# Neighbourhood attention with projections one step ahead instead of two, and rotated queries of the first layer written directly into their tile

## The chip, the core and the metric

One core of a Trainium2 chip runs the whole program. The metric is the device time of one execution in microseconds (us). Five engines work side by side, each with its own queue of instructions that it runs strictly in order: PE (TensorE, matrix products into PSUM), DVE (VectorE), ACT (ScalarE), POOL (GpSimd) and SP (SyncE, which here issues the DMAs). An instruction that waits on a semaphore holds back all that stands behind it on its engine.

## The reference, cut to what matters

Two layers of a backbone over 1024 latent tokens and 256 context tokens, width 1024, all in float32. The first layer runs differential attention (8 heads; each with two query/key halves of 64 columns, values of 128) beside a short convolution. The second runs two-dimensional neighbourhood attention beside a gated linear attention. What the change touches is this:

```python
q = apply_rope(aq.reshape(bsz, seq, *qk_shape), cos, sin)      # layer 0, latent tokens only
q = cp[2].reshape(bsz, clen, *qk_shape)                        # layer 0, context tokens: no rotation
...
s_loc = einsum(q_r, k_band) * scale + bias                     # layer 1: 8 rows x 16 columns around each query
s_ctx = einsum(q_r, kc) * scale                                # and all 256 context keys
p = softmax(concat([s_loc, s_ctx]))
out = p_loc @ v_band + p_ctx @ vc
```

In layer 1 the queries, keys and values are projections `h @ w_in` of the normed tokens, 16 heads of 64 columns.

## The kernel before, in words

**Matmul in pieces.** A float32 operand is split into a high part and a rest (`whi`/`wlo` for weights by `split_w`, L241 on ACT and L242 mostly on POOL; `hA`/`hB` for tokens), and a product is the sum of three products. A projection unit turns 128 columns of weights over all tokens; it has a step for each chunk of tokens (512, 512, 256). A step is `proj_chunk` (L438): 24 matmuls into one of two PSUM banks called `pj`, which the step's `use` function then empties.

**The stream.** `Stream` holds all projection units of the program in order. Attention code asks it for steps between its own pieces: `ws.run(n)` issues n steps, `ws.until(name)` all up to a named one, `ws.open(gate)` needs all before a gate to be done. So attention (many short, dependent pieces on four engines) and projections (long, independent PE work) are interleaved. The Tile scheduler then orders the instructions of each engine by priority and readiness, so a piece may move some way from where the code put it.

**Layer 0, the rotation.** At the start of a head `diff_head` calls `ws.until("v..")`, which runs the projections of keys, queries and values one after the other. For keys and queries `rope` (L514) copies the PSUM bank into a scratch tile `ropex` (L519, ACT), swaps lanes (L521, DVE), multiplies by cosine (L522, DVE) and sine (L523, POOL) and adds (L524, DVE, into the scratch tile). `use_q` (L538) then copies the scratch to the query tile `qf` (L543, POOL), for all three chunks; the context chunk is only scaled, not rotated. The first scores of the head need `qd`, the split queries (L581 on ACT, L582 and L583 on DVE), which read `qf`.

**Layer 1, neighbourhood attention.** `na` walks over 64 units: 8 pairs of heads i, 2 heads m in each, 4 blocks bp of 256 queries. For a unit, `scores` builds the split queries `nqd` (L1459 on ACT, L1461 and L1462 on DVE) from the projected queries `nq` (L1393), multiplies with the keys into PSUM (`NS`, L1473 and L1474, twice, once for each 128 queries), adds the bias and takes the maximum (`np`, L1477 on DVE), exponentiates (L1479, ACT), takes the reciprocal (L1480, DVE) and scales (L1481, POOL). `values` transposes the weights (`ntr`, L1522, PE), splits them (`pth` L1531 on ACT, `ptl` L1532 on DVE) and multiplies with the values (`nav`, L1499); the last sum of a unit is `nu` (L1505, DVE). The order in the code is: scores of unit n+1, values of unit n, then one projection step for the pair i+1 (keys `ck` 3 steps, values `cv` 3, queries `cq` 2: 8 steps for 8 units). Ahead of the loop stands `ws.run(2)`. On POOL the same stretch has also the bias tiles `nB` (L1433), the copies of the keys `nk` (L1387), the gate product `nu` (L1546) after each pair and `wlo` (L242) once for each unit of weights. After unit 53 the projections have run out; the steps of the output projection (`ops`, L756) come with unit 59.

Of the kernel before, what the change touches and what calls it, by code (L numbers as in the profile page):

```python
# [10 lines left out]
F32 = mybir.dt.float32  # L11
F32R = mybir.dt.float32r
AF = mybir.ActivationFunctionType
ALU = mybir.AluOpType
# [4 lines left out]
P = 128  # L19
D = 1024  # L20
NK = D // P
SEQ = 1024
CTX = 256
TOK = SEQ + CTX
# [74 lines left out]
class Kernel:  # L99
# [411 lines left out]
        rope_es.close()  # L511
        return conv_es

    def rope(self, ps, t0, tn, scale):  # L514

        nc = self.nc
        big = self.ap.tile([P, 1280], F32, name="ropex", tag="p0", bufs=2)
        x, s = big[:, 0:tn], big[:, 640:640 + tn]
        nc.scalar.mul(out=x, in_=ps, mul=scale) if scale != 1.0 else nc.scalar.copy(out=x, in_=ps)  # L519
        if t0 < SEQ:  # L520
            nc.vector.stream_shuffle(s, x, [i ^ 16 for i in range(32)])  # L521
            nc.vector.tensor_tensor(out=x, in0=x, in1=self.cos[:, t0:t0 + tn], op=ALU.mult)  # L522
            nc.gpsimd.tensor_tensor(out=s, in0=s, in1=self.sin[:, t0:t0 + tn], op=ALU.mult)  # L523
            nc.vector.tensor_tensor(out=x, in0=x, in1=s, op=ALU.add)  # L524
        return x, s

    def use_k(self, h, ci, t0, tn, ps):
# [8 lines left out]
            nc.vector.tensor_tensor(out=self.kst[m][64:128, t0:t0 + tn], in0=x[half], in1=hi[half], op=ALU.subtract)  # L536

    def use_q(self, h, ci, t0, tn, ps):  # L538
        nc, ap = self.nc, self.ap
        if ci == 0:  # L540
            self.qf = ap.tile([P, TOK], F32, name="qf", tag="qf")
        x, _ = self.rope(ps, t0, tn, 0.125)
        nc.gpsimd.tensor_copy(self.qf[:, t0:t0 + tn], x)  # L543

    def use_v(self, h, ci, t0, tn, ps):
        nc, ap = self.nc, self.ap
# [892 lines left out]
    def na(self):  # L1439
        nc, ap, ws = self.nc, self.ap, self.ws  # L1440
# [108 lines left out]
        bias[0] = self.na_bias(0)  # L1549
        units = [(i, m, bp) for i in range(8) for m in range(2) for bp in range(4)]  # L1550
        nxt = scores(*units[0])
        ws.run(2)
        for n, (i, m, bp) in enumerate(units):
            ps_ = nxt
            if bp == 1 and 2 * i + m < 15:
# [93 lines left out]
```

## Time and profile before

| | |
|---|---|
| Median of 3 runs | 3112.27 us (3111.68 to 3113.80) |
| The profiled execution | 3112.84 us, its span 3111.1 us |
| Busy share of the span | PE 95%, DVE 61%, ACT 49%, POOL 31% |
| Mean granted TensorE clock | 0.985 |
| Layer 0's attention | about 140 to 1400 us |
| Neighbourhood attention | about 2300 to 2940 us |

PE is busy nearly throughout, so the end moves when PE's idle time does, when its instructions become fewer, or when its clock changes. The views below are read for PE's idle time: how much of it lies in the two stages that the change touches, and what ended each stretch of it.

### The profile page before, as it was taken

What the parts mean: (1) busy time and instruction counts of PE and PEld (TensorE: products, weight loads), DVE (VectorE), ACT (ScalarE), POOL (GpSimd) and SP (SyncE); (2) the same over time, 40 slices, a digit from 0 to 9 for tenths busy, and PEclk for the clock granted to TensorE, in tenths of its full rate; (3) what the DMA queues carried; (4) which work ended last, traced back from release to release, by engine and by line L of the source; (5) the groups of instructions that cost most, each with busy time, mean ns of one, the idle gap of its engine ahead of it and who ended that gap; (6) DMA issues with size and microseconds to landing.
All of it is one profiled execution on the core that took longest, in us unless ns stands there. A gap on an engine that the chain in (4) does not pass through costs nothing. (4 is left out here: it accounts for less than half of the span.)

```text
span 3111.1 us, 42394 instructions
## 1 busy us (share of the span) xinstructions
PE 2948.6 (95%) x16244; PEld 2463.5 (79%) x16244; DVE 1890.8 (61%) x3157; ACT 1523.8 (49%) x2821; POOL 972.7 (31%) x765
## 2 busy tenths in 40 slices
PE   6999999999999999999999999999999999998898
PEld 4888888888888887888787787878777777777786
DVE  5675757575665657564245757575847666667723
ACT  4553535353544454444345665555635554555621
POOL 3212131313121211215333232222336545555622
PEclk9999999999999999999999999999999999999999
DMA  6111110211110201125432112121121111112323
GB/s 226 34 45 48 48 51 29 64 35 58 35 58 28 72 28 56 36 63 192 136 124 73 51 44 66 58 62 55 55 71 38 44 37 38 43 43 98 102 90 122
DMA packets 236982, 206.53 MB, mean 66 GB/s; under 512 B 43591, under 2 KB 194538, under 8 KB 236778
## 3 DMA queue, kind: packets, MB, share of 16 engines
q1 hardware_dynamic: 236778, 203.81, 21.2%
q8 instruction: 128, 2.10, 0.3%
q14 instruction: 76, 0.62, 0.1%
HBM read 168.10 MB, written 35.67 MB: 65 GB/s over the span
## 5 line engine op out<-in xcount | busy, mean ns | idle before, releaser
L242 POOL TENSOR_TENSOR wlo<-wraw,whi 128x1024 fp32r<-128x1024 f32 x149 | 368.8, 2475 | 1164.1 <-ACT whi L241 1045.0
L438 PE MATMUL pj<-hBh,whi 128*128 128x512 f32 (+1 forms) x1712 | 386.2, 354 | 8.2 <-ACT hBh L353 4.8
L438 PE MATMUL pj<-hBl,whi 128*128 128x512 f32 (+1 forms) x1712 | 364.4, 348 | 0.9 <-DVE hBl L354 0.9
L438 PE MATMUL pj<-hBh,wlo 128*128 128x512 f32 (+1 forms) x1712 | 348.1, 344 | 0.0
L241 ACT CAST whi<-wraw 128x1024 fp32r<-128x1024 f32 x176 | 184.7, 1049 | 318.0 <-PE ops L756 188.6
L438 PEld LDWEIGHTS pj<-hBh,whi 128*128 128x128 f32 x1712 | 276.8, 192 | 42.4 <-ACT hBh L353 5.4
L438 PEld LDWEIGHTS pj<-hBl,whi 128*128 128x128 f32 x1712 | 279.4, 191 | 36.8 <-DVE hBl L354 1.1
L438 PEld LDWEIGHTS pj<-hBh,wlo 128*128 128x128 f32 x1712 | 277.2, 190 | 37.2
L438 PE MATMUL pj<-hAh,whi 128*128 128x512 f32 x968 | 283.1, 414 | 14.7 <-ACT ropex L519 13.0
L438 PE MATMUL pj<-hAl,whi 128*128 128x512 f32 x968 | 255.4, 396 | 0.0
L594 DVE TENSOR_REDUCE st<-S 128x1 f32<-128x1280 f32 (+1 forms) x160 | 203.9, 1274 | 79.0 <-PE S L592 79.0
L438 PE MATMUL pj<-hAh,wlo 128*128 128x512 f32 x968 | 250.4, 397 | 0.0
L596 ACT ACTIVATE p<-S,st 128x1280 f32<-128x1280 f32 (+1 forms) x160 | 186.0, 1163 | 81.9 <-DVE st L594 80.4
L1481 POOL TENSOR_TENSOR np<-np,nst 128x640 f32<-128x640 f32 x128 | 168.1, 1315 | 143.5 <-DVE nst L1480 79.9
L438 PEld LDWEIGHTS pj<-hAh,wlo 128*128 128x128 f32 x968 | 182.4, 190 | 37.5
L438 PEld LDWEIGHTS pj<-hAh,whi 128*128 128x128 f32 x968 | 173.4, 194 | 48.5 <-ACT ropex L519 14.4
L438 PEld LDWEIGHTS pj<-hAl,whi 128*128 128x128 f32 x968 | 180.5, 191 | 35.7 <-issue 0.4
L592 PE MATMUL S<-kst,qd 128*128 128x512 f32 (+1 forms) x832 | 192.2, 360 | 0.2 <-ACT p L596 0.2
L1477 DVE CUSTOM_DVE_ANT_0 np<-NS,nB 128x640 f32<-128x640 f32 x128 | 105.0, 820 | 115.0 <-PE NS L1474 96.3
L592 PEld LDWEIGHTS S<-kst,qd 128*128 128x128 f32 x832 | 137.0, 188 | 40.3 <-ACT p L596 21.5
L617 ACT CAST ath<-atr 128x512 fp32r<-128x512 f32 (+1 forms) x208 | 99.1, 505 | 113.4 <-PE atr L614 112.8
L1531 ACT CAST pth<-ntr 128x512 fp32r<-128x512 f32 (+2 forms) x224 | 101.2, 461 | 84.2 <-PE ntr L1522 46.4
(361 smaller groups left out, 6266.5 us busy)
## 6 DMA issues: line engine op xcount, KB each, us to landing
wraw<-in_ev_w_in_dram SPq DMA_DIRECT2D x64, 512.0 KB, 4.0
wraw<-in_od_w_in_dram SPq DMA_DIRECT2D x56, 512.0 KB, 3.8
wraw<-in_w_out_dram SPq DMA_DIRECT2D x55, 512.0 KB, 3.8
wraw<-in_w_mod_dram SPq DMA_DIRECT2D x48, 512.0 KB, 3.6
sgT<-gt SPq DMA_DIRECT2D x32, 256.0 KB, 2.3
uT<-sg SPq DMA_DIRECT2D x8, 640.0 KB, 3.5
nG<-in_rpbp_dram SPq DMA_DIRECT2D x128, 40.0 KB, 2.2
xt<-in_x_dram SPq DMA_DIRECT2D x8, 512.0 KB, 6.6
```

What stands on the lines that cost most here:

```text
L241: nc.scalar.copy(out=hi, in_=u.raw)
L242: (nc.vector if u.lo_eng == "v" else nc.gpsimd).tensor_tensor(out=lo, in0=u.raw, in1=hi.bitcast(F32), op=ALU.subtract)
L438: nc.tensor.matmul(ps[:, 0:tn], lhsT=a[:, k, :], rhs=self.h_at(k, t0, tn)[b], start=n == 0, stop=n == 23)
L592: nc.tensor.matmul(S[:, c0:c0 + tn], lhsT=qd[:, 2 * m + part, P * qt:P * qt + P], rhs=self.kst[m][:, t0:t0 + tn], start=part == 0, stop=pa ...
L594: nc.vector.tensor_reduce(out=st[:, m:m + 1], in_=S[:, 0:n], axis=AX.X, op=ALU.max, negate=True)
L596: nc.scalar.activation(out=p[m][:, 0:n], in_=S[:, 0:n], func=AF.Exp, bias=st[:, m:m + 1], accum_out=st[:, 2 + m:3 + m])
L617: nc.scalar.copy(out=dh, in_=tv)
L1477: nc.vector.tensor_tensor_reduce(out=p, in0=S[:, z0:z0 + 640], in1=bias[2 * i + m][:, c0:c0 + 640], scale=1.0, scalar=3e38, op0=ALU.add, o ...
L1481: nc.gpsimd.tensor_tensor(out=p, in0=p, in1=st[:, 2:3].broadcast_to([P, 640]), op=ALU.mult)
L1531: nc.scalar.copy(out=hv[:, s:e], in_=tr[:, s:e])
```

## The change

In layer 0, `rope` takes an optional output. For rotated chunks the last addition on DVE writes its result straight to `qf`; the context chunk is scaled by ACT from PSUM straight into `qf`, with no scratch tile. The 24 POOL copies (three chunks, eight heads) are gone. In layer 1, `ws.run(2)` ahead of the loop becomes `ws.run(1)`, so each of the 56 projection steps is issued one unit later.

```diff
-    def rope(self, ps, t0, tn, scale):
+    def rope(self, ps, t0, tn, scale, out=None):
         nc = self.nc
+        if out is not None and t0 >= SEQ:
+            nc.scalar.mul(out=out, in_=ps, mul=scale)
+            return
...
-            nc.vector.tensor_tensor(out=x, in0=x, in1=s, op=ALU.add)
+            nc.vector.tensor_tensor(out=x if out is None else out, in0=x, in1=s, op=ALU.add)
         return x, s
...
     def use_q(self, h, ci, t0, tn, ps):
-        nc, ap = self.nc, self.ap
         if ci == 0:
-            self.qf = ap.tile([P, TOK], F32, name="qf", tag="qf")
-        x, _ = self.rope(ps, t0, tn, 0.125)
-        nc.gpsimd.tensor_copy(self.qf[:, t0:t0 + tn], x)
+            self.qf = self.ap.tile([P, TOK], F32, name="qf", tag="qf")
+        self.rope(ps, t0, tn, 0.125, self.qf[:, t0:t0 + tn])
...
         nxt = scores(*units[0])
-        ws.run(2)
+        ws.run(1)
         for n, (i, m, bp) in enumerate(units):
```

**Order, first place.** POOL's queue in layer 0, around the projections of the second head (before, then after; line numbers move by 1 to 3):

```order
L523 TENSOR_TENSOR ropex<-ropex,sin 128x512 x2
L242 TENSOR_TENSOR wlo<-wraw,whi 128x1024
L523 TENSOR_TENSOR ropex<-ropex,sin 128x512
L543 COPY qf<-ropex 128x512
L523 TENSOR_TENSOR ropex<-ropex,sin 128x512
L543 COPY qf<-ropex 128x512
L543 COPY qf<-ropex 128x256
L242 TENSOR_TENSOR wlo<-wraw,whi 128x1024 x6
```

```order
L684 TENSOR_TENSOR cacc<-cacc,csg 128x256
L526 TENSOR_TENSOR ropex<-ropex,sin 128x512 x2
L242 TENSOR_TENSOR wlo<-wraw,whi 128x1024
L526 TENSOR_TENSOR ropex<-ropex,sin 128x512 x2
L242 TENSOR_TENSOR wlo<-wraw,whi 128x1024 x6
```

The three copies are gone, and the next weight split follows the last sine product directly.

**Order, second place.** PE's queue in neighbourhood attention, where the scores of a new pair of heads begin (the first `NS` with a new key tile). Before, the last query projection (`pj<-hBh,wlo 128x512 x8`) stands 25 rows ahead of the first row here; these are the last rows of the next pair's first key projection, and then the scores:

```order
L438 MATMUL pj<-hAh,whi 128x512
L438 MATMUL pj<-hAl,whi 128x512 x8
L438 MATMUL pj<-hAh,wlo 128x512 x8
L1473 MATMUL NS<-nk_20347,nqd 128x384
L1474 MATMUL NS<-nk_20347,nqd 128x256
```

After, the first row here is the end of the last query projection itself:

```order
L438 MATMUL pj<-hBh,wlo 128x512 x8
L1523 MATMUL ntr<-ident,np 128x128 x4
L1500 MATMUL nav<-pth,nv 128x256 x2
L1500 MATMUL nav<-ptl,nv 128x256 x2
L1523 MATMUL ntr<-ident,np 128x128 x4
L438 MATMUL pj<-hAh,whi 128x512 x3
L1523 MATMUL ntr<-ident,np 128x128 x2
L438 MATMUL pj<-hAh,whi 128x512 x3
L1474 MATMUL NS<-nk_20379,nqd 128x384
L1475 MATMUL NS<-nk_20379,nqd 128x256
```

Between the queries' projection and their first use there was a whole projection step of 24 matmuls and other work; now there are six projection matmuls, ten transposes and four products with the values. There are seven such places (pairs 1 to 7).

**Order, third place.** POOL's queue at the end of a pair, around the gate product `nu` (before, then after):

```order
L1481 TENSOR_TENSOR np<-np,nst 128x640 x2
L1387 CAST nk_21172<-nkh 64x512
L1387 CAST nk_21173<-nkh 64x512
L1481 TENSOR_TENSOR np<-np,nst 128x640
L242 TENSOR_TENSOR wlo<-wraw,whi 128x1024
L1481 TENSOR_TENSOR np<-np,nst 128x640
L1546 TENSOR_TENSOR nu<-nu,nsg 128x512 x2
```

```order
L1482 TENSOR_TENSOR np<-np,nst 128x640 x2
L1547 TENSOR_TENSOR nu<-nu,nsg 128x512 x2
L1388 CAST nk_21204<-nkh 64x512
L1388 CAST nk_21205<-nkh 64x512
L1535 MEMSET pth 128x256
L1536 MEMSET ptl 128x256
L1482 TENSOR_TENSOR np<-np,nst 128x640 x2
L242 TENSOR_TENSOR wlo<-wraw,whi 128x1024
```

The weight split stood between the two `np` products of one unit; it now stands behind both of a later unit.

## Rows read from the trace of the kernel before

**Rows 1.** Windows by stage: length, busy us of each engine, granted clock, DMA
```profile
core 0: us, PE busy (x) PEld busy (x) DVE busy (x) ACT busy (x) POOL busy (x), PEclk, DMA share, GB/s
140.00:1400.00 1260.00, 1246.03 (x7162) 1042.09 (x7161) 799.73 (x1278) 601.45 (x969) 246.60 (x129) 1.00 0.16 47
2300.00:2860.00 560.00, 508.96 (x2947) 433.43 (x2947) 366.81 (x740) 285.93 (x609) 293.78 (x311) 0.98 0.17 44
2860.00:2940.00 80.00, 68.49 (x395) 56.23 (x394) 70.17 (x134) 56.26 (x118) 59.85 (x51) 0.96 0.29 101
```
**Rows 2.** PE's waits, 130 to 1400 us: us in total, times, longest
```profile
PE pj L438 <- ACT ropex L519: 13.0, 7, 5.3
```
**Rows 3.** Timeline, 215 to 282 us: start, us, engine, operation [idle before]
```profile
247.68 2.40 POOL L242 TENSOR_TENSOR wlo<-wraw,whi 128x1024 fp32r<-128x1024 f32 x1
247.75 2.87 DVE L524 TENSOR_TENSOR ropex<-ropex 128x512 f32<-128x512 f32 x1 [1.19 <-POOL ropex L523]
...
257.75 0.69 DVE L524 TENSOR_TENSOR ropex<-ropex 128x512 f32<-128x512 f32 x1 [1.18 <-POOL ropex L523]
...
258.51 0.61 POOL L543 COPY qf<-ropex 128x512 f32<-128x512 f32 x1 [0.79 <-DVE ropex L524]
...
259.15 1.69 ACT L581 CAST qd<-qf 64x256 fp32r<-64x256 f32 x4 [4.89 <-POOL qf L543]
...
260.86 0.60 ACT L519 ACTIVATE ropex<-pj 128x512 f32<-128x512 f32 x1
...
261.51 2.11 PE L438 MATMUL pj<-hAh,whi 128*128 128x512 f32 x8 [1.29 <-ACT ropex L519]
...
265.86 0.69 DVE L524 TENSOR_TENSOR ropex<-ropex 128x512 f32<-128x512 f32 x1 [1.18 <-POOL ropex L523]
...
269.27 0.69 DVE L559 TENSOR_TENSOR vl<-vtr,vh 128x512 fp32r<-128x512 f32 x1 [2.72 <-ACT vh L558]
```
**Rows 4.** PE's waits, 2300 to 2860 us
```profile
PE nav L1499 <- DVE ptl L1532: 20.0, 13, 1.8
PE nav L1499 <- DVE nu L1505: 16.9, 25, 1.8
...
PE NS L1473 <- DVE nqd L1462: 2.2, 1, 2.2
```
**Rows 5.** Timeline, 2558 to 2579 us
```profile
2558.12 1.98 PE L438 MATMUL pj<-hBh,wlo 128*128 128x512 f32 x8
2559.93 0.35 PE L1473 MATMUL NS<-nk,nqd 128*128 128x384 f32 x1
...
2560.55 0.60 PE L1522 MATMUL ntr<-ident,np 128*128 128x128 f32 x4
...
2560.91 0.37 PE L1499 MATMUL nav<-pth,nv 128*128 128x256 f32 x1
...
2566.11 2.46 POOL L242 TENSOR_TENSOR wlo<-wraw,whi 128x1024 fp32r<-128x1024 f32 x1 [0.34 <-ACT whi L241]
...
2566.42 2.44 DVE L1462 CAST nqd<-nqd 64x512 fp32r<-64x512 f32 x1
...
2569.55 0.39 PE L1499 MATMUL nav<-ptl,nv 128*128 128x256 f32 x1 [1.84 <-DVE ptl L1532]
...
2570.43 0.76 PE L1522 MATMUL ntr<-ident,np 128*128 128x128 f32 x5 [0.49 <-POOL np L1481]
...
2575.91 0.42 DVE L1462 CAST nqd<-nqd 64x512 fp32r<-64x512 f32 x1
...
2577.30 0.48 PE L1499 MATMUL nav<-pth,nv 128*128 128x256 f32 x2 [1.78 <-DVE nu L1505]
```
**Rows 6.** Groups by line and shape, DVE, 2400 to 2800 us: busy, mean ns
```profile
L1462 DVE CAST nqd<-nqd 64x512 fp32r<-64x512 f32 x39 | 40.9, 1050 | 1.3
L1461 DVE TENSOR_TENSOR nqd<-nq,nqd 64x256 fp32r<-64x256 f32 x39 | 35.2, 904 | 0.9
```
**Rows 7.** The same for ACT
```profile
L1459 ACT CAST nqd<-nq 64x256 fp32r<-64x256 f32 x40 | 26.1, 653 | 4.3 <-PE NS L1474 3.5
...
L1393 ACT ACTIVATE nq<-pj 128x512 f32<-128x512 f32 x10 | 6.0, 599 | 24.6 <-PE pj L438 24.6
```

## The prediction

> **What bounds the kernel now.** I read the page's table of engines first: PE is busy for 95% of the span, no other engine for more than 61%. So the question for each edit is which idle time of PE it takes away or adds. The windows by stage [rows 1] tell how much there is: in layer 0's attention PE stands idle for 1260 − 1246.03 = 14 us in all, in neighbourhood attention for 560 − 508.96 = 51 us, in its last 80 us for 11.5 us. Nothing that the change does in layer 0 can give more than 14 us. The granted clock is 1.00 in layer 0 and 0.98 in neighbourhood attention, the upper of its two levels nearly throughout, and the change adds and takes no matmul, so I price no change of clock. Then I read what ended PE's idle time in the two stages [rows 2, 4], and last the timelines around the places whose order moves [rows 3, 5]. In layer 0, 13.0 of the 14 us end with one event: ACT empties a PSUM bank for the rotation (L519) and PE's next projection step may start [rows 2]. In neighbourhood attention the largest waits are of the products with the values, for DVE's `ptl` (20.0 us) and `nu` (16.9 us) [rows 4].
>
> **Layer 0: the copies.** Removed are 24 POOL copies of 0.61 us; POOL is busy for 246.60 of 1260 us there [rows 1], so their own time is worth nothing. What counts is whom they held up. The reader is to follow head 2 [rows 3]: DVE's addition ends at 257.75 + 0.69 = 258.44; POOL copies until 259.12; ACT, which had waited 4.89 us for that copy, starts `qd` at 259.15 and holds its queue for 1.69 us; behind it stands the emptying of a PSUM bank (260.86, 0.60 us), and PE starts at 261.51 after 1.29 us of waiting. Without the copy ACT can start at 258.44 plus the same hand-over of 0.03 to 0.07 us, about 258.48, which is 0.67 us sooner, and all behind it moves with it. The wait occurs 7 times; the longest, 5.3 us, is in a head whose DVE is late for other reasons, so it stays. The other six are 13.0 − 5.3 = 7.7 us, 1.28 each. Term: 6 × 0.67 = −4.0 us; bounds 0 (ACT then waits for something else) and −7.7 (all six go). The context chunk, scaled by ACT straight into `qf`, costs the same ACT instruction as before.
>
> The edit has a price too. POOL's next weight split `wlo` stood behind the copies and now follows the last sine product, so it can start when the second addition of a head does (265.86). A row shows what that meeting costs: at 247.75 the addition lay beside a `wlo` of 2.40 us and took 2.87 us instead of 0.69 [rows 3], 2.18 more. I take it at nothing, since DVE then idles 2.72 us before its next instruction at 269.27 [rows 3], which covers it. If the cover is gone it is 2.18 × 7 = +15.3 us.
>
> The Trainium skill (page "SBUF — State Buffer", section "Who interferes with whom") says that a DVE instruction with two SBUF inputs contends with a GpSimd instruction that reads SBUF, and that whoever starts first keeps the shared ports for the whole instruction. The row of 2.87 against 0.69 us agrees. By that rule alone, with no cover, the change would lose the 15.3 us in layer 0, and it is the fourth rival below.
>
> **Neighbourhood attention: the weight split moves.** Before, once in each pair, `wlo` stands on POOL between the two `np` products of a unit. The reader is to see one of the six such places, 82 us apart [rows 5]: `wlo` at 2566.11 for 2.46 us, beside it DVE's last step of the split queries, 2.44 us where it takes 0.42 at 2575.91; and then PE waits 1.84 us for `ptl` (behind that step on DVE), 0.49 for the second `np` (behind `wlo` on POOL) and 1.78 for `nu` (behind on DVE), 4.1 us together. After, `wlo` stands behind both `np` of a later unit. Bounds: 0 (it meets DVE's work of the next unit just as badly) and 6 × 4.1 = −24.6. The grouped row says how likely another meeting is: this cast has a mean of 1050 ns over 39 instructions, against 0.42 us alone [rows 6], so many more of them than the six are held up by other POOL work; a `wlo` has no free place in this stage where DVE isn't met. But the `np` that PE and DVE need next is no longer behind it. I take half: 6 × 2.05 = −12.3 us.
>
> **Neighbourhood attention: the queries come late.** At seven places the last query projection stood a whole step (24 matmuls) and more ahead of the scores of the new pair; now six projection matmuls, ten transposes and four products stand between. The chain from the projection's end to the first score is ACT `nq` 0.60, ACT cast 0.65, DVE subtraction 0.90, DVE cast 1.05 [rows 6, 7], 3.2 us, and ACT finishes on average one other such piece first (0.6): 3.8 us. The cover on PE: eight projection matmuls last 2559.93 − 2558.12 = 1.81 us, so six last 1.36; four transposes 0.36, so ten 0.90; a second product with the values adds 0.48 − 0.37 = 0.11, so four 0.44 [rows 5]; 2.7 us in all. Exposed: 1.1 us, 7 × 1.1 = +7.7 us. Behind the waiting `NS` on PE stand the transposes of the unit before and the next projection step, so they wait with it; DVE and ACT, which feed those transposes, gain a little ground meanwhile. Bounds: 0 (ACT and DVE are free at once, and the scheduler's matmuls cover it) and the nearest row, the one wait of `NS` for `nqd` that the stage shows, 2.2 us [rows 4], at all seven: +15.4. The 24 × 1.81/8 = 5.4 us of cover taken away say that more than this would have to be found on DVE and ACT, not on PE.
>
> **Tail.** One projection step is done a unit later, so the stretch without projections from 2866 us on, where PE idles for 11.5 us and DVE is busy for 70.17 of 80 [rows 1], is a unit shorter. A step is 5.4 us of PE's work; bounds 0 and −5.4. DVE, not the lack of matmuls, sets that stretch for the larger part, so I take the lower half: −2.
>
> At the start of the stage the `ws.run(1)` itself costs nothing: PE has the same order up to about 2344 us, since the projections fill the time until the first bias tile.
>
> **Sum**: −4.0 − 12.3 + 7.7 − 2 = −10.6 us. The profiled execution took 3112.84 us, 0.57 above the median of the runs: 3112.27 − 10.6 = 3101.7, rounded 3102.
>
> **Rivals.** What a measurement of this kernel can tell from no change is about 0.2%, 6.2 us: faster is below 3106.0, slower above 3118.5.
>
> 1. Only layer 0 counts: the scheduler orders by readiness, so the three terms of neighbourhood attention cancel, and its waits for `ptl` and `nu` (36.9 us of the 51 [rows 4]) stand for DVE's total load, 366.81 of 560 us, which the change leaves as it is. Against it: the cluster of 4.1 us hangs visibly on one instruction in one place. −4.0 gives 3108, same.
>
> 2. Slower: the queries come too late. At each new pair PE waits for `nqd` behind ACT's and DVE's other casts, 2.2 us, and `wlo` finds DVE elsewhere: 15.4 − 4.0 = +11.4, 3124. It decides from a wait of (6.2 + 4.0)/7 = 1.46 us per place on, if the cluster stays. For it: my own estimate has 1.1 us exposed, and DVE's cast varies from 0.42 to 2.44 us. Against it: only one such wait stands in the stage before, so DVE and ACT usually keep up.
>
> 3. The cluster goes entirely, since both `np` products now come ahead of `wlo`: −4.0 − 24.6 + 7.7 − 2 = −22.9, 3089. Against it is the mean of 1050 ns: DVE is met in other places too.
>
> 4. In layer 0 the addition is held by `wlo` in seven heads and nothing covers it: the sum above + 15.3 = +4.7, 3117; half of that chance lies above the bound for slower. Against it are the 2.72 us that DVE idles.
>
> **Chances.** The forecast 0.45, rival 1 0.24, rival 2 0.14, rival 3 0.12, rival 4 0.05. Faster: 0.45 + 0.12 = 0.57. Same: 0.24 + 0.03 = 0.27. Slower: 0.14 + 0.02 = 0.16. The forecast's own range, from the halves of its terms, is 3095 to 3108; with rivals 1, 3 and 4 the range is 3088 to 3118, which leaves out rival 2 and the outer edges.
>
> **What would show it.** In the profile after, the waits of `pj` for ACT's `ropex` (or for the context's scaling) should add up to about 9 instead of 13 us, and DVE's second addition of a head may grow to 2.9 us without PE waiting for it. In neighbourhood attention the group of three waits behind `wlo` (4.1 us) should have shrunk to about 2, while seven new waits of `NS` for `nqd` of about 1 us appear; PE's idle time in the last 80 us should be near 9. The prediction is wrong if the `NS` waits exceed 1.5 us each, if the waits for `ptl` and `nu` grow because `wlo` now holds DVE ahead of them, or if the idle time of layer 0 rises above 14 us.

## The result, and the profile after

| | before | after |
|---|---|---|
| Median | 3111.97 us (4 runs) | 3072.73 us (4 runs, 3070.42 to 3073.53) |
| Ratio to before, 95% interval | | 0.9874 [0.9861, 0.9886] |
| The profiled execution, its span | 3112.84 us, 3111.1 us | 3072.52 us, 3070.7 us |

The kernel became faster by 39.2 us (1.3%), where 10.6 had been forecast. The direction was right, the size was not, and the time lies 15 us below the range.

To see where the time went, cut both traces at the same instructions. From the last transposition of the first tokens to the last score of layer 0, and from the first to the last `NS` of neighbourhood attention, the windows of the kernel before are (length, busy us of each engine with its instructions, granted clock, DMA share, GB/s):

```profile
84.90:1376.10 1291.20, 1274.80 (x7333) 1066.95 (x7332) 825.05 (x1313) 619.42 (x1003) 260.70 (x140) 1.00 0.15 46
2303.13:2928.72 625.59, 565.48 (x3267) 479.84 (x3268) 428.19 (x856) 333.94 (x710) 344.22 (x352) 0.98 0.18 50
```

The same two stretches after:

```profile
84.60:1370.00 1285.40, 1273.74 (x7332) 1066.29 (x7331) 840.23 (x1313) 619.07 (x1003) 248.72 (x117) 1.00 0.16 46
2296.45:2888.55 592.10, 560.23 (x3274) 474.62 (x3275) 412.45 (x856) 335.38 (x711) 339.07 (x353) 0.99 0.20 53
```

Layer 0 is 1291.20 − 1285.40 = 5.8 us shorter, neighbourhood attention 625.59 − 592.10 = 33.5 us, and all else 1.1 of the span's 40.4. In neighbourhood attention PE's idle time (length less busy) fell from 60.1 to 31.9 us, which is 28.2 of the 33.5. The other 5.3 are busy time for the same work, at a granted clock of 0.99 instead of 0.98. What share of those 5.3 the change has made is open: e1 below, with the projections as before, has 563.4 us of busy time in this stretch, between the 565.5 of the kernel before and the 560.2 of the changed one. DVE's busy time fell by 15.7 us with the same 856 instructions: it is held up less often.

What ended PE's waits after, in layer 0 (130 to 1400 us; the row of [rows 2]) and then in neighbourhood attention (2300 to 2860 us; the rows of [rows 4]):

```profile
PE pj L438 <- ACT ropex L522: 9.0, 7, 5.4
```

```profile
PE ntr L1523 <- POOL np L1482: 8.7, 13, 2.0
PE NS L1474 <- DVE nqd L1463: 7.9, 7, 2.3
PE nav L1500 <- DVE nu L1506: 6.1, 21, 1.1
...
PE nav L1500 <- DVE ptl L1533: 0.9, 2, 0.6
```

The two large waits of before, 20.0 us for `ptl` and 16.9 for `nu`, are 0.9 and 6.1 now. The waits of `NS` for `nqd` are there, seven of them, 7.9 us: six of 0.92 and, at the last new pair, one of 2.3.

**Where the waits stood.** The timeline of PE shows them place by place. This is one pair in the kernel before, from 2488 to 2570 us; only rows in which PE waited are shown, and the last group of the pair, at 2569.55 to 2577.30, stands in [rows 5]:

```profile
2495.97 0.47 PE L1499 MATMUL nav<-pth,nv 128*128 128x256 f32 x2 [1.49 <-DVE nu L1505]
...
2506.82 0.38 PE L1499 MATMUL nav<-ptl,nv 128*128 128x256 f32 x1 [1.58 <-DVE ptl L1532]
...
2516.22 0.48 PE L1499 MATMUL nav<-pth,nv 128*128 128x256 f32 x2 [0.26 <-DVE nu L1505]
...
2533.45 0.51 PE L1499 MATMUL nav<-pth,nv 128*128 128x256 f32 x2 [0.17 <-DVE nu L1505]
...
2542.45 0.66 PE L1522 MATMUL ntr<-ident,np 128*128 128x128 f32 x4 [0.64 <-DVE ptl L1532]
...
2545.14 0.51 PE L1499 MATMUL nav<-pth,nv 128*128 128x256 f32 x2 [0.86 <-DVE nu L1505]
```

And this is all that one pair has after (2474 to 2550 us):

```profile
2474.69 0.50 PE L1500 MATMUL nav<-pth,nv 128*128 128x256 f32 x2 [0.25 <-DVE nu L1506]
...
2477.59 0.55 PE L1523 MATMUL ntr<-ident,np 128*128 128x128 f32 x3 [0.61 <-POOL np L1482]
...
2482.40 0.51 PE L1500 MATMUL nav<-pth,nv 128*128 128x256 f32 x2 [0.18 <-DVE nu L1506]
...
2501.77 0.48 PE L1500 MATMUL nav<-pth,nv 128*128 128x256 f32 x2 [0.28 <-DVE nu L1506]
...
2528.48 0.43 PE L1474 MATMUL NS<-nk,nqd 128*128 128x384 f32 x1 [0.92 <-DVE nqd L1463]
```

Before, there were three groups of waits in a pair. Group A is that of [rows 5], 4.1 us (the largest of the six places, whose mean is 3.8); the 1.49 at 2495.97 is the end of the pair before's. Group B is the 1.58 at 2506.82. Group C is 0.64 and 0.86 at 2542 to 2545. After, A is down to 0.25 + 0.61 + 0.18 = 1.0, B and C are gone, and 0.92 for the late queries is new. The change in a pair is −3.1 − 1.6 − 1.5 + 0.9 = −5.3 us; the distance from pair to pair, read at the weight split in the same place, fell from 82 us (2519.68 to 2600.96 to 2683.33) to 75.9 (2505.00 to 2580.87 to 2656.73).

What stands beside B and C is to be seen on the other engines. POOL and DVE in the kernel before, around group B and then around group C:

```profile
2502.87 0.94 POOL L1433 TENSOR_TENSOR nB<-namask,nG 128x384 f32<-128x384 bf16 x1 [1.47 <-DVE nst L1480]
...
2503.77 1.25 POOL L1481 TENSOR_TENSOR np<-np,nst 128x640 f32<-128x640 f32 x1
...
2503.89 1.52 DVE L1461 TENSOR_TENSOR nqd<-nq,nqd 64x256 fp32r<-64x256 f32 x1
...
2504.98 1.17 POOL L1433 TENSOR_TENSOR nB<-namask,nG 128x384 f32<-128x384 bf16 x1
...
2505.63 0.81 DVE L1462 CAST nqd<-nqd 64x512 fp32r<-64x512 f32 x1
...
2539.03 2.39 POOL L242 TENSOR_TENSOR wlo<-wraw,whi 128x1024 fp32r<-128x1024 f32 x1 [3.74 <-PE pj L438]
...
2540.42 1.38 DVE L1461 TENSOR_TENSOR nqd<-nq,nqd 64x256 fp32r<-64x256 f32 x1
...
2543.22 0.95 POOL L1433 TENSOR_TENSOR nB<-namask,nG 128x384 f32<-128x384 bf16 x1 [1.31 <-DVE nst L1480]
2543.25 1.20 DVE L1462 CAST nqd<-nqd 64x512 fp32r<-64x512 f32 x1
```

In both places POOL is at work just when DVE splits the queries, and DVE's subtraction takes 1.38 to 1.52 us and its cast 0.81 to 1.20, where they take about 0.6 and 0.42 alone. At B the subtraction lies beside a product `np`, which had stood behind a bias tile `nB` in POOL's queue, and the cast beside the next `nB`; at C the subtraction lies beside the weight split and the cast beside an `nB`. DVE's `ptl` and `nu` stand behind that, and PE behind them.

At B that meeting is still there in the changed kernel, as long as before:

```profile
2482.52 1.25 POOL L1482 TENSOR_TENSOR np<-np,nst 128x640 f32<-128x640 f32 x1
...
2482.70 1.47 DVE L1462 TENSOR_TENSOR nqd<-nq,nqd 64x256 fp32r<-64x256 f32 x1
...
2483.46 1.55 PE L438 MATMUL pj<-hAl,whi 128*128 128x512 f32 x6
2483.74 1.18 POOL L1434 TENSOR_TENSOR nB<-namask,nG 128x384 f32<-128x384 bf16 x1
...
2484.39 0.81 DVE L1463 CAST nqd<-nqd 64x512 fp32r<-64x512 f32 x1
...
2484.84 1.98 PE L438 MATMUL pj<-hAh,wlo 128*128 128x512 f32 x8
```

What is gone is PE's wait. PE had done all of the unit's products with the values by 2483.46 and has 14 projection matmuls to run while DVE is late; before, two projection matmuls (2504.61) stood between those products and the last one, which needs the late `ptl` (2506.82). At C it is the split of the new pair's queries that POOL met. After, these queries are projected later, and DVE's split of them starts at 2526.29: its first subtraction still lies beside a weight split (POOL, 2524.61) and takes 1.10 us, but the bias tiles are done by then, and PE's only wait there is the one of 0.92 for the late queries.

### The profile page after: what moved, and what is told of

It reads as the page before. It is cut to its first block, busy times and chain, and to the rows that moved or that the text cites. A ratio compares the mean times of both kernels' runs of the same rounds, so it can differ in the third digit from the quotient of the medians.

```text
span 3070.7 us, 42345 instructions
## 1 busy us (share of the span) xinstructions
PE 2936.1 (96%) x16244; PEld 2453.3 (80%) x16244; DVE 1891.3 (62%) x3157; ACT 1523.6 (50%) x2821; POOL 953.8 (31%) x741
## 5 line engine op out<-in xcount | busy, mean ns | idle before, releaser
L242 POOL TENSOR_TENSOR wlo<-wraw,whi 128x1024 fp32r<-128x1024 f32 x149 | 368.7, 2475 | 1157.7 <-ACT whi L241 1049.6
L438 PEld LDWEIGHTS pj<-hBh,whi 128*128 128x128 f32 x1712 | 275.2, 191 | 43.2 <-ACT hBh L353 5.4
L1533 DVE TENSOR_TENSOR ptl<-ntr,pth 128x512 fp32r<-128x512 f32 (+2 forms) x224 | 117.8, 536 | 50.2 <-ACT pth L1532 45.9
```

Of the source, the lines that this page charges most:

```text
L242: (nc.vector if u.lo_eng == "v" else nc.gpsimd).tensor_tensor(out=lo, in0=u.raw, in1=hi.bitcast(F32), op=ALU.subtract)
L438: nc.tensor.matmul(ps[:, 0:tn], lhsT=a[:, k, :], rhs=self.h_at(k, t0, tn)[b], start=n == 0, stop=n == 23)
L1533: nc.vector.tensor_tensor(out=lv[:, s:e], in0=tr[:, s:e], in1=hv[:, s:e].bitcast(F32), op=ALU.subtract)
```

## The experiments

All were timed in three rounds beside the kernel before, whose medians then were 3111.2 to 3112.0 us. The units of a pair are counted 0 to 7 (units 0 to 3 are the first head's four query blocks); a pair's projection steps are keys (512, 512, 256 tokens), values (512, 512, 256), queries (512, 512). With two steps ahead the short steps of 256 tokens come in units 0 and 3, with one ahead in units 1 and 4.

**The edit of layer 0 alone**

```diff
-        ws.run(1)
+        ws.run(2)
```

> The changed kernel with the two steps ahead put back, so that only the edit of layer 0 is left. The trace of the changed kernel has layer 0's attention 5.8 us shorter (its waits for ropex fell from 13.0 to 9.0 us). If the two parts add, 3106 us. If the edit of layer 0 is worth only its 4.0 us of waits, 3108. If the parts need each other, further from both than 3 us.

3106.02 us, 0.9979 [0.9969, 0.9988]. With the shift undone, layer 0 alone gives 5.9 us, as its window in the trace said (5.8), and the remaining 33.3 are the shift's. All three groups of waits are back in this trace.

**Two ahead, no weight split on POOL**

```diff
+        if u.name[:2] in ("ck", "cv", "cq") and u.name[2:] in "1234567":
+            u.hl = (hi.rearrange("p (k n) -> p k n", n=u.width),) * 2
+            return
```

> Two steps ahead, and the weight split of POOL (wlo) is left out for the weights of neighbourhood attention in pairs 1 to 7: the high part is used in its place, so the products are as many but the low part of these weights is missing from the result. Collision theory (the loss came from wlo standing between the two np products and holding DVE): the three waits of 4.1 us per pair go with it, 3076 to 3084 us. Cover theory (the loss came from the short projection steps of 256 tokens falling on units that need the most cover): 3098 to 3106.

3080.68 us, 0.9899 [0.9884, 0.9914]: 25.3 less than with it, as the collision theory had it. PE's waits in one pair (2485 to 2557 us):

```profile
2488.27 0.39 PE L1503 MATMUL nav<-ptl,nv 128*128 128x256 f32 x1 [1.61 <-DVE ptl L1536]
...
2526.22 0.47 PE L1503 MATMUL nav<-pth,nv 128*128 128x256 f32 x2 [1.10 <-DVE nu L1509]
...
2549.94 0.55 PE L1526 MATMUL ntr<-ident,np 128*128 128x128 f32 x3 [0.86 <-POOL np L1485]
```

Group B is untouched (1.61), C is 1.10, and of group A 0.86 for `np` and a wait of 0.25 for `nu` are left.

**Two ahead, the short steps moved**

```diff
-            yield self.proj(f"ck{i}", ..., CHUNKS, ...)
+            yield self.proj(f"ck{i}", ..., CHUNKS, ..., order=[2, 0, 1] if i else None)
```

(the same for the values)

> Two steps ahead, but the short step (256 tokens) of the keys and of the values comes first of its three instead of last, so that it falls on units 6 and 1 of a pair's eight (query blocks in the middle) and not on 0 and 3 (blocks at the edge); the weight splits keep their units. Cover theory: 3072 to 3085 us. Collision theory: 3100 to 3108.

3082.52 us, 0.9905 [0.9890, 0.9920]: 23.5 less than e1, inside the range that the cover theory gave. One pair (2476 to 2528 us), and the cast and the weight split ahead of it:

```profile
2467.83 0.42 DVE L1463 CAST nqd<-nqd 64x512 fp32r<-64x512 f32 x1
...
2472.30 2.40 POOL L242 TENSOR_TENSOR wlo<-wraw,whi 128x1024 fp32r<-128x1024 f32 x1
...
2479.68 0.63 PE L1523 MATMUL ntr<-ident,np 128*128 128x128 f32 x2 [0.52 <-DVE ptl L1533]
...
2486.76 0.38 PE L1500 MATMUL nav<-ptl,nv 128*128 128x256 f32 x1 [1.52 <-DVE ptl L1533]
...
2524.82 0.66 PE L1523 MATMUL ntr<-ident,np 128*128 128x128 f32 x4 [0.67 <-DVE ptl L1533]
...
2527.49 0.50 PE L1500 MATMUL nav<-pth,nv 128*128 128x256 f32 x2 [0.94 <-DVE nu L1506]
```

A has shrunk to 0.52 and a wait of 0.25 for `nu`, and B (1.52) and C (0.67 + 0.94) stay. But the edit did not leave the weight split where it was, as the expectation had it: in e1 one split of each pair starts 4.2 us ahead of the next gate product, between the two `np` and beside the cast, which takes 2.43 us; here it starts 2.5 us behind the gate product, and the cast takes 0.42. So this run takes away the short step and the meeting at once, and doesn't tell which of them counts. In e2 the split alone is taken away, with the short step where it was, and that nearly ends A.

**One ahead, the short steps put back on units 0 and 3**

The changed kernel with `order=[0, 2, 1]` for keys and values.

> One step ahead, but the short step of keys and of values comes second of its three, so that it falls on units 0 and 3 again, where the kernel before had it; all else is as in the changed kernel. Cover theory: the gain is given back, 3095 to 3106 us. Collision theory: 3070 to 3077, as the changed kernel.

3084.73 us, 0.9911 [0.9896, 0.9925]: 12.0 us of the gain are given back, about a third; the time lies between the ranges of the two theories. A pair has

```profile
2470.65 0.55 PE L1523 MATMUL ntr<-ident,np 128*128 128x128 f32 x3 [0.90 <-POOL np L1482]
...
2477.18 0.48 PE L1500 MATMUL nav<-pth,nv 128*128 128x256 f32 x2 [1.57 <-DVE nu L1506]
...
2532.71 0.43 PE L1474 MATMUL NS<-nk,nqd 128*128 128x384 f32 x1 [0.94 <-DVE nqd L1463]
```

A returns in part (0.90 and 1.57), with the gate product beside it (POOL, 2470.55 and 2472.62) and the weight split elsewhere (2481.24). So a short step there has a price of its own. B and C don't return.

**Three ahead**

```diff
-        ws.run(1)
+        ws.run(3)
```

> Three steps ahead (the layer 0 edit kept). Theory of position (what counts is which unit's work a step, its weight split and the bias tiles meet; the amount ahead is not the point): the short steps fall on units 7 and 2, the place where short step, weight split and gate product met is taken apart, and the 0.92 us wait of NS at each new pair is gone: 3070 to 3092 us. Rival (less ahead is better by itself: one ahead 3073, two ahead 3106): 3106 or more.

3086.25 us, 0.9915 [0.9901, 0.9930]. Less ahead isn't better by itself: three beats two by 20 us. Two is the worst of the three tried in this order of the projections.

**One ahead, no weight split**

The edit of e2 on the changed kernel.

> One step ahead as in the changed kernel, and POOL's weight split left out for the weights of pairs 1 to 7 (the high part used in its place, so their low part is missing from the result). With two steps ahead this gave 25 us. If the split costs only where it meets the short step, it costs almost nothing here (the np waits of about 0.6 us a pair): 3065 to 3073 us. If it costs by its load on DVE wherever it stands: 25 us again, 3045 to 3055.

3073.70 us, 0.9877 [0.9862, 0.9892], the same as the changed kernel. The same work that cost 25 us with two ahead costs nothing here. It is not its load that counts but what it meets and whether PE then waits.

**Two ahead, no bias tiles**

```diff
-                bias[2 * i + m + 1] = self.na_bias(2 * i + m + 1)
+                bias[2 * i + m + 1] = bias[2 * i + m] if i else self.na_bias(2 * i + m + 1)
```

> Two steps ahead, and the bias tiles of heads 3 to 15 are left out (the tile of head 2 is used for them, so POOL's nB and the DMAs of nG are missing from pairs 1 to 7, and the result has the wrong bias). Theory: two of the three groups of waits in a pair (1.58 for ptl; 0.64 for ptl and 0.86 for nu) come from nB standing between the np products beside DVE's nqd; they go, 3.1 us x 7 = 21 us, 3082 to 3088. Rival (they come from DVE's nqd standing ahead of ptl, whatever POOL does): 3100 to 3106.

3095.76 us, 0.9948 [0.9933, 0.9963]: 10.3 us, half of what was expected. One pair (2486 to 2533 us):

```profile
2487.29 0.48 PE L1500 MATMUL nav<-pth,nv 128*128 128x256 f32 x2 [1.78 <-DVE nu L1506]
2496.93 0.39 PE L1500 MATMUL nav<-ptl,nv 128*128 128x256 f32 x1 [0.39 <-DVE ptl L1533]
...
2532.60 0.66 PE L1523 MATMUL ntr<-ident,np 128*128 128x128 f32 x4 [0.66 <-DVE ptl L1533]
```

B is down from 1.58 to 0.39 and the second half of C is gone, so with two ahead these need `nB`. The first half of C stays at 0.66: beside it stands the weight split (2539.03 in the rows of before above), and without that (e2) it is gone. A is as before in this pair; over the six pairs its third wait varies from 0.64 to 1.78.

**Two ahead, neither**

> Two steps ahead, without POOL's weight split in pairs 1 to 7 and without the bias tiles of heads 3 to 15 (both left out as before, so the result lacks them). Alone the first gave 25.3 us and the second 10.3 us against the kernel with two steps ahead (3106.0). If the groups of waits are separate places on PE, they add: 3070 us, within 4. If both lift the same load of POOL on DVE, the second adds little: 3076 to 3081.

3062.81 us, 0.9846 [0.9831, 0.9861]: 43.2 us less than e1, against 35.6 for the sum of the two, and 3 us below the range that was expected if they add. PE's idle time does add: from the first to the last `NS` it is 60.9 us in e1, 42.4 in e2, 47.2 in e9 and 29.6 here, which is 18.4 and 13.6 alone and 31.3 together (with both left out the largest wait of the pair from 2475 to 2553 us is 0.87). The rest lies elsewhere: PE's busy time in that stretch is 563.4 us in e1, 556.1 in e2, 567.4 in e9 and 556.3 here, and the first `NS` starts 6.5 us earlier than in e1, ahead of all that was edited. What POOL's two kinds of work cost with two ahead is more than the whole gain of the shift; what the bias tiles cost with one ahead was not run.

**One ahead, the short step of the values first**

The changed kernel with `order=[2, 0, 1]` for the values alone.

> One step ahead as in the changed kernel, but the short step of the values comes first of its three, so it falls on unit 2 (a middle block) and not on unit 4 (an edge block). If edge units need the longer step's cover: 3064 to 3071 us. If unit 4 had no wait to lose: 3071 to 3078.

3078.47 us, 0.9888 [0.9872, 0.9905]. No gain but 5.7 us more than the changed kernel: unit 4 had no wait to lose, and a new one of 0.94 for `ptl` appears. That an edge block needs the longer step's cover is not borne out.

**Queries before values, one ahead and none**

```diff
-            yield self.proj(f"cv{i}", ...)
             yield self.proj(f"cq{i}", ...)
+            yield self.proj(f"cv{i}", ...)
```

> One step ahead, with the projections of a pair in the order keys, queries, values, so that the queries are there three steps before the scores of the new pair (the values are needed later); to make room the value scratch has a tile of its own, its 256-column part shares the keys' scratch, and nG shares the buffers of np. The wait of NS for nqd at each new pair (0.92 us x 7 = 6.4) should go: 3066 us if the weight splits and the short step of the values (now on unit 6) meet nothing new. Rival by the theory of position: they do meet a bias tile or a gate product, and it is 3075 to 3090.

> The same order of projections with no step ahead (each step a unit later again; the last value step then stands behind the scores of the new pair, which don't need it). If less ahead is better by itself: below the one with one ahead by 10 us or more. By the theory of position it may go either way: the short steps fall on units 2 and 7, the weight splits on 0, 3 and 5; 3066 to 3092 us.

One ahead: 3074.60 us, 0.9883 [0.9868, 0.9897], the same as the changed kernel, where 3066 was forecast. The seven waits of `NS` for `nqd` are gone from the list of waits, which shows that they come from the late queries. Waits for `ptl` and `np` came in their place (up to the sixth pair none over 0.47 us); the last pair takes longer. None ahead: 3091.63 us, 0.9938 [0.9921, 0.9955]; a wait of 2.34 us for `np` stands in a pair. With e5 this is the second sign that the amount ahead isn't what counts.

**The output projection opened earlier**

```diff
-            if n == len(units) - 5:
+            if n == len(units) - 8:
...
-                ws.run(1 if n < len(units) - 5 else 2)
+                ws.run(1)
```

> The changed kernel with the output projection opened after unit 56 instead of 59 (its steps then come one per unit). In the changed kernel PE idles 13.8 us between the gate product of pair 5 and the last score, in a stretch without projections from unit 55 on. If PE lacks other work there: half of it, 3066 us, and the waits for nu, np and ptl in the stretch shrink. If the stretch is set by DVE (95.5 of 117.4 us busy), or the loading of the gated rows is late: 3071 to 3076.

3077.61 us, 0.9895 [0.9879, 0.9912]: no gain, and a little above both ranges. The edit didn't do what it was for: the first matmul of the output projection (`ops`) starts 58.6 us behind the gate product of pair 5 in both traces, and up to the last `NS` there are 609 matmuls in place of 605. So whether PE lacks other work there stays untested. No version that computes the whole reference beat the changed kernel.

## Why the prediction was right or wrong

**Layer 0, right.** The waits for `ropex` are 9.0 us, as forecast, and in head 2 the order of things is the one described. Timeline of the changed kernel, 257 to 268 us:

```profile
257.33 0.69 DVE L527 TENSOR_TENSOR qf<-ropex 128x512 f32<-128x512 f32 x1 [1.19 <-POOL ropex L526]
258.06 1.69 ACT L582 CAST qd<-qf 64x256 fp32r<-64x256 f32 x4 [4.21 <-DVE qf L527]
...
259.77 0.60 ACT L522 ACTIVATE ropex<-pj 128x512 f32<-128x512 f32 x1
...
260.42 2.11 PE L438 MATMUL pj<-hAh,whi 128*128 128x512 f32 x8 [0.61 <-ACT ropex L522]
...
264.70 2.40 POOL L242 TENSOR_TENSOR wlo<-wraw,whi 128x1024 fp32r<-128x1024 f32 x1
264.78 2.88 DVE L527 TENSOR_TENSOR qf<-ropex 128x512 f32<-128x512 f32 x1 [1.19 <-POOL ropex L526]
```

ACT starts `qd` straight behind DVE's addition, PE's wait is 0.61 instead of 1.29 us [rows 3], 0.68 less where 0.67 was expected. The measured 5.8 us hold, beside the 4.0 of these waits, another 1.1 of shorter busy time and 0.7 of idle time elsewhere that no row was sought for.

**The fourth rival's price was right, and so was its cover.** `wlo` does meet the second addition: 2.88 us at 264.78, 0.69 before [rows 3]. DVE's busy time in the stretch of layer 0 rose from 825.05 to 840.23, which is 15.2 us and was put at 15.3. PE waits for none of it: DVE's idle time covered it. The Trainium skill (page "SBUF — State Buffer", section "Who interferes with whom") has the rule that a DVE instruction with two SBUF inputs is held by a GpSimd instruction that reads SBUF and started first, for its whole length. This row agrees, and the rule priced without the cover, as in the fourth rival (+4.7 us), would have had the wrong sign of the result.

**Late queries, right.** 7.9 us in seven waits, forecast 7.7, and e11, which brings the queries earlier, ends them. The agreement of the sums is in part luck: six places have 0.92 us, under the 1.1 forecast, and the last has 2.34, over the 1.5 that the prediction named as a sign of being wrong. Rival 2's decisive 1.46 us per place was not reached on average. The one wait of 2.2 in [rows 4], which the prediction took as its nearest row, is the first score of the whole stage (2303.13); it is there after too (2.53 us at 2296.45, outside the list above), so all seven are new.

**The tail, small and nearly right.** Between the gate product of pair 5 and the last score PE's idle time was 14.8 us before (113.05 − 98.28 from 2815.65) and is 13.8 after (117.40 − 103.60 from 2771.20), −1.0 where −2 was forecast. Whether it is short of matmuls, e13 couldn't show.

**The weight split, wrong: this is the step that failed.** The term of −12.3 was half of one group of waits. Two things were off. First, group A went not by half but from 4.1 to 1.0. The prediction explained A by `wlo` between the two `np` alone, which e2 bears out for most of it (4.1 to 1.1), and argued by DVE's mean cast that `wlo` would meet DVE elsewhere just as badly. It does meet DVE elsewhere (one subtraction in each pair takes 1.10 us beside it in the changed kernel), and e8 shows that this costs nothing: PE doesn't wait behind it. A short step in the place of A has a price of its own (e4); what the split would cost there beside a long step, no run shows. Second, groups B and C, 3.1 us in a pair, were in no term. With two ahead they need `nB` (e9), and one half of C `wlo` (e9 against e2). The diff touches `nB` nowhere, but a shift of the projections by one unit changes what PE has to run when DVE is late (B, where `nB` still meets the queries) and when the queries are split (C). Three groups per pair fall by 6.2 us, where 2.05 was taken.

The numbers to see this were at hand. The waits for `ptl` and `nu` add up to 36.9 us [rows 4], and the six clusters explained 24.6 of PE's 51 us of idle time in that stage [rows 1]. The rest was put down to "DVE's total load, which the change leaves as it is" (rival 1). It wasn't the number of DVE's instructions: the same 856 left PE 32 us idle instead of 60. Rival 3, which let all of A go, was nearest with 3089 and lacked B and C.

**The clock.** It was priced at nothing. PE's busy time in neighbourhood attention fell 5.3 us at a granted clock of 0.99 instead of 0.98. The trace shows where it was lost before. These are two microseconds right behind the wait for `ptl` in group A, at the start of the pair shown above (1.79 us at 2487.33) and at its end (1.84 at 2569.55); the number behind POOL's count is the granted clock:

```profile
2488.00:2490.00 2.00, 1.79 (x7) 1.70 (x8) 1.18 (x4) 0.80 (x3) 2.00 (x3) 0.50 0.77 229
2570.00:2572.00 2.00, 1.57 (x10) 1.39 (x11) 1.53 (x4) 0.93 (x3) 2.00 (x3) 1.00 0.88 243
```

Right behind that wait of about 1.8 us the clock fell to its lower level (0.50, 1.2 GHz) in four of the six pairs and stayed at the upper one in two; in the changed kernel it stays at the upper level in all pairs but the last ones, where waits of 2.34 and 1.98 us stand. So fewer long waits gave back a little more than their own length. How much of the 5.3 is the change's is open, as said above.

**What stays open.** Why with two ahead PE's last product of the unit at B stands so close behind the late `ptl`, and with one ahead behind 14 projection matmuls, is an outcome of the scheduler's order that no run took apart; that PE's order is what ends B is read from the rows, not tried. e9 shows that B and half of C need the tiles with two ahead, not which instruction would have to move. Nor is it known whether the split in the place of A would have cost anything beside a long step, or why e10's first score comes 6.5 us earlier than e1's.

## What to carry to other kernels

When an engine is busy throughout but for short waits, list its waits place by place over one period of the loop until they add up to its idle time, and price every group, not only that at which the order visibly moves. A shift of a filler stream by one unit moves the whole pattern of what meets what: try the neighbouring offsets (here 3106, 3073 and 3086 us for two, one and three ahead) instead of arguing from "more ahead is safer". A slow instruction on a side engine costs only where the main engine has too little else to run before it needs the result (the same meeting cost 1.58 us in one order and nothing in the other), so look at what stands between the two on the main engine, and not only at the meeting. And check in the trace that an edit moved what it was meant to move, and nothing else: e3 moved the weight split as well, e13 moved almost nothing.

## What the runs showed of the hardware

DVE's addition of 128x512 took 0.69 us alone and 2.86 to 2.88 beside a POOL subtraction of 128x1024 (2.40 us) that had started up to 0.08 us ahead of it; POOL's took no longer for it. Seven more such meetings added 15.2 us to DVE's busy time and none to the end. Leaving out 21 such POOL subtractions was worth 25.3 us in one order of the program and nothing (3073.70 against 3072.73 us) in another. The granted clock of PE fell to 0.50 right behind a wait of about 1.8 us in four of six like places of one execution (1.79 us, then 0.50 from 2488 to 2490) and not in the other two (1.84 us, then 1.00 from 2570 to 2572).
